# Layer 1 attention: first value block as three float32r products, normalisation on ScalarE, the token tile in two halves

## The chip, the cores and the metric

The kernel runs on one core of one Trainium2 chip, in one launch. The time is the device time of that core in microseconds (us), and the number compared is a median over runs. Before the change it is 2091.49 us, the median of three runs (2091.32 to 2092.57).

## The reference

A decoder trunk of two layers on 256 tokens of 2048 float32 features. Layer 0 mixes tokens with a block-sparse attention (at this length plain causal attention, 16 heads of 128), layer 1 with a latent attention ("MLA"), and each is followed by a gated feed-forward block with a short causal convolution:

```python
for i in range(DEPTH):                      # DEPTH = 2
    h = rms_norm(x, attn_norm[i])
    y = moba_attention(h, ...) if i == 0 else mla_attention(h, ...)
    x = x + y
    h = rms_norm(x, ffn_norm[i])
    x = x + conv_glu_ffn(h, ...)

def mla_attention(h, ...):
    cq = rms_norm(h @ wq_a, g_qa)                 # 512
    q = (cq @ wq_b).reshape(B, S, H, NOPE + RD)   # 16 heads, 128 + 64
    ckv = rms_norm(kv_a[..., :512], g_kva)        # kv_a = h @ wkv_a
    kv = (ckv @ wkv_b).reshape(B, S, H, NOPE + VD)
    s = (q_nope @ k_nope + q_rope @ k_rope) * scale   # per head, causal
    p = softmax(s)
    o = p @ v                                     # this product is changed
    return o.reshape(B, S, H * VD) @ wo
```

What the change touches is the softmax's last step (the division by the row sums) and the product of the probabilities with v, in layer 1 only, and where some tiles lie in SBUF.

## The kernel before

**Weights.** All weights stream through one class, `Stream`. A piece is 128x512 float32; 1480 pieces arrive in 370 units of up to four by transfers on SyncE's queue (L71), three units ahead. For each piece ScalarE makes a rounded float32r part `whi` (L104) and VectorE the rest `wlo = raw - whi` (L105). Five buffers of each exist, and in the steady state a piece is split four quanta before TensorE uses it.

**Quanta.** The program is a list of quanta, one for each weight piece: TensorE's products of that piece. A product of two float32 matrices is done as three float32r products (high by high, high by low, low by high). In token-major quanta (`tok_major`, L237) six products of 512 columns use the activations as the stationary operand and the weights as the moving one. In feature-major quanta (`feat_major`, L263 to L265) twelve products of 256 columns have it the other way round.

**Order.** The order is written out by hand. The last loop (L1086 to L1092) issues for each quantum: the splits of the piece four quanta on, the quantum's products, then `leading` work (values, then transposes of heads), then the `side` work planned for that quantum, in the order in which it was planned. Every engine runs its instructions in that order, so a late instruction delays all that stands behind it on its engine.

**Layer 1 attention.** Four groups of four heads. Each group has projections of four quanta each (k, q, v; the first group q, the rotary part, k, v), then four heads, three quanta apart. `Head.plan` (L554) puts a head's steps on quanta: at q `scores` on TensorE and `biased` on VectorE (mask and row maximum), at q+1 `exps` on ScalarE with row sums, at q+2 `normal` (a VectorE reciprocal, L509, and two VectorE multiplications, L511), at q+6 `turn` (three TensorE transposes, L519) and `turned` (the copy out of PSUM), at q+9 `values` (TensorE) and `parted` (the output as high and low part, L551 and L552, in `oT`). For the last head the steps come at q+5 and q+7.

In layer 1 before the change, `turned` is one ScalarE copy of 128x384 (L525) and `values` is two float32 products: 256 columns for the first block of keys (L544) and 128 columns for the second (L545). A float32 product stands in the trace as two MATMULs. Layer 0 (`parts=True`) already has the other form: `turned` is a float32r copy of the first block (L531), a float32 copy of the second (L532) and a VectorE subtraction for the low part (L533); `values` is three float32r products (L462 to L464) and one float32 product (L542).

**Tiles.** The normalised tokens are one tile `h` of 16 rows of 512 (high and low part). In layer 1, once the projections have read it, its place is taken by `room`, one tile with the queries, the keys, the values and the rotary key `kr` of layer 1. The values come from PSUM by two ScalarE copies of 128x512 for a group (L619, in `evac_values`).

Of the kernel before, what the change touches and what calls it, by code (L numbers as in the profile page):

```python
# [10 lines left out]
F32 = mybir.dt.float32  # L11
F32R = mybir.dt.float32r
BF16 = mybir.dt.bfloat16
AF = mybir.ActivationFunctionType
ALU = mybir.AluOpType
PSUM = bass.MemoryType.PSUM

P = 128
S = 256
D = 2048  # L20
NT = S // P
KD = D // P
# [28 lines left out]
H_START = 8  # L51


class Stream:
# [55 lines left out]

    def take(self, i):
        return self.parts.pop(i)


@with_exitstack
def trunk(ctx: ExitStack, tc: tile.TileContext, a, out):
    nc = tc.nc
    const = ctx.enter_context(tc.tile_pool(name="const", bufs=1))
    keep = ctx.enter_context(tc.tile_pool(name="keep", bufs=1))
# [8 lines left out]
    mm = nc.tensor.matmul  # L128
# [35 lines left out]
    att_pool = att.enter_context(tc.tile_pool(name="att", bufs=2))  # L164
# [50 lines left out]
    def at(q, f, *args):  # L215
        side.setdefault(q, []).append((f, args))
# [7 lines left out]
    def add(f, *args):  # L224
        quanta.append((f, args))
        return len(quanta) - 1
# [41 lines left out]
    class Norm:  # L268
# [3 lines left out]
        def __init__(self, gain_col, spread):  # L272
            self.gain_col, self.spread = gain_col, spread
            self.h, self.sq = None, {}

        def high(self, j):
            if self.h is None:
                t = keep.tile([P, KD * 2 * S + 64], F32R, name="h")
                self.h = t[:, H_START : H_START + KD * 2 * S].rearrange("p (k s) -> p k s", k=KD)
            g = par[:, self.gain_col + j : self.gain_col + j + 1]  # L280
            nc.scalar.activation(self.h[:, j, :S], xT[:, j, :], AF.Copy, scale=g)  # L281

# [177 lines left out]
    def three(o, w_hi, w_lo, m_hi, m_lo, start, stop):  # L460

        mm(o, w_hi, m_hi, start=start, stop=False)  # L462
        mm(o, w_hi, m_lo, start=False, stop=False)  # L463
        mm(o, w_lo, m_hi, start=False, stop=stop)  # L464


    class Head:
        def __init__(self, h, qT, kT, v, i, oT, scale, rope=None, parts=False):
            self.h, self.qT, self.kT, self.v, self.i = h, qT, kT, v, i
            self.oT, self.scale, self.rope, self.parts = oT, scale, rope, parts  # L470

        def scores(self):
            sc = ps_sc.tile([P, 512], F32, name="sc")
# [34 lines left out]
        def normal(self):  # L508
            nc.vector.reciprocal(self.st[:, 6:8], self.st[:, 4:6])  # L509
            for c, n, k in ((0, P, 0), (P, S, 1)):  # L510
                nc.vector.tensor_scalar(  # L511
                    self.s[:, c : c + n], self.s[:, c : c + n], self.st[:, 6 + k : 7 + k], None,
                    op0=ALU.mult,
                )
# [5 lines left out]
            self.tp = tp  # L520

        def turned(self):
            if not self.parts:
                self.pT = att_pool.tile([P, 3 * P], F32, name="pT", bufs=2)
                nc.scalar.copy(self.pT, self.tp[:, : 3 * P])  # L525
                return

            self.pT = att_pool.tile([P, 2, S], F32R, name="pT", bufs=2)
            self.pT1 = att_pool.tile([P, P], F32, name="pT1", bufs=2)
            hi, lo = self.pT[:, 0], self.pT[:, 1]  # L530
            nc.scalar.copy(hi, self.tp[:, :S])  # L531
            nc.scalar.copy(self.pT1, self.tp[:, S : 3 * P])  # L532
            nc.vector.tensor_tensor(lo, self.tp[:, :S], hi.bitcast(F32), op=ALU.subtract)  # L533

        def values(self):
            o = ps_sc.tile([P, 512], F32, name="sc")
            v = self.v()
            vs = slice(self.i * P, (self.i + 1) * P)
            if self.parts:
                v0, v1 = v  # L540
                three(o[:, :S], v0[:, 0, vs], v0[:, 1, vs], self.pT[:, 0], self.pT[:, 1], True, False)
                mm(o[:, P:S], v1[:, vs], self.pT1, start=False, stop=True)  # L542
            else:
                mm(o[:, :S], v[:, 0, vs], self.pT[:, :S], start=True, stop=False)  # L544
                mm(o[:, P:S], v[:, 1, vs], self.pT[:, S:], start=False, stop=True)  # L545
            self.o = o

        def parted(self):
# [22 lines left out]
    env = {}  # L571
# [32 lines left out]
    def evac_parts(state, key, scale):  # L604
        v0, v1 = env[key]
        hi, lo = v0[:, 0], v0[:, 1]
        first_, second = (state["acc"][t][:, :512] for t in range(NT))
        r = scale()
        nc.scalar.activation(hi, first_, AF.Copy, scale=r[:, 0:1])
        nc.vector.scalar_tensor_tensor(  # L610
            lo, first_, r[:, 0:1], hi.bitcast(F32), op0=ALU.mult, op1=ALU.subtract
        )
        nc.scalar.activation(v1, second, AF.Copy, scale=r[:, 1:2])

    def evac_values(state, key, scale):
        for t in range(NT):
            dst, src = env[key][:, t, :], state["acc"][t][:, :512]
            if scale is None:
                nc.scalar.copy(dst, src)  # L619
            else:  # L620
                nc.scalar.activation(dst, src, AF.Copy, scale=scale()[:, t : t + 1])

    def plan_heads(q, hs, key, step, out=None, late=0, wide=False):

# [30 lines left out]
    for g in range(4):  # L655
        for kind in "qkv":
            state = {"first": g == 0 and kind == "q"}
            for kt in range(KD):
                q = add(tok_major, state, lambda: n1.h, kt, KD - 1)
# [228 lines left out]

    def kr_rotate(t):
        if t == 0:  # L890
            env["krr"] = att_pool.tile([P, NT, 2, 64], F32, name="krr", bufs=1)
        x = env["ckv"][:, t, 512:]
        nc.vector.scalar_tensor_tensor(
            x, x, env["kvr"][:, 2 * t + 1 : 2 * t + 2], gains[:, G_KR : G_KR + 64],
            op0=ALU.mult, op1=ALU.mult,
        )
        ct = tab[:, T_LC + t * 64 : T_LC + (t + 1) * 64]
        st = tab[:, T_LS + t * 64 : T_LS + (t + 1) * 64]
        t1 = att_pool.tile([P, 64], F32, name="kro1", bufs=2)
        t2 = att_pool.tile([P, 64], F32, name="kro2", bufs=2)  # L900
        nc.vector.tensor_tensor(t1, x, ct, op=ALU.mult)
        nc.vector.tensor_tensor(t2[:, :32], x[:, 32:], st[:, :32], op=ALU.mult)
        nc.vector.tensor_tensor(t2[:, 32:], x[:, :32], st[:, 32:], op=ALU.mult)
        for i in range(2):
            nc.vector.tensor_tensor(env["krr"][:, t, i], t1, t2, op=ALU.add)
# [56 lines left out]
    for r in range(4):  # L962
        state = {}
        for kq in range(4):
            q = add(lambda t_hi, t_lo, n, st=state, kq=kq: feat_major(
                st, lambda: n3.h, 4 * kq, KD - 1, kq == 0, t_hi, t_lo, n))
# [52 lines left out]
    for half in range(2):  # L1019
        state = {}  # L1020
        for kt in range(KD):
            q = add(tok_major, state, lambda: n3.h, kt, KD - 1)
# [1 line left out]
        at(q + (0 if half else 1), kva_squares, half)  # L1024

    def open_room():
        t = keep.tile([P, KD * 2 * S + 64], F32, name="room", tag="h")
        env["room"] = t[:, : 32 * S].rearrange("p (k s) -> p k s", k=32)
        env["kr"] = [env["room"][:, 28 + i] for i in range(2)]

    at(q, open_room)
    at(q, kva_rstd)
# [4 lines left out]
    for t in range(NT):  # L1037
        at(q + 9 + t, kr_rotate, t)
    at(q + 13, kr_turn)

    def mla_tiles(g):
        i = 4 * (g % 2)
        env["qT", g] = env["room"][:, i : 4 + i]
        env["kT", g] = env["room"][:, 8 + i : 12 + i]
        i = 4 * (g % 3)
        env["v", g] = env["room"][:, 16 + i : 20 + i].rearrange("p (t c) s -> p t (c s)", t=NT)

    for g in range(4):
        for kind in "kqv" if g else "qrkv":
            if kind == "r":  # L1050
                rotary_queries(1, (6, 8, 10, 11, 12, 15, 16, 18, 19, 21, 22, 24, 25, 27, 28, 31, 32))
                continue
            state = {}
            for kt in range(4):
                q = add(tok_major, state, lambda kind=kind: env["cqT" if kind == "q" else "ckvT"], kt, 3)
            if kind == ("k" if g else "q"):
                at(q, mla_tiles, g)
            if kind == "v":
                at(q, evac_values, state, ("v", g), None)
            else:  # L1060
                q_q = q
                hs = Heads(state, 4, P, None, 0, None, (lambda: cq["scale"]) if kind == "q" else None,
                           C_GQN if kind == "q" else C_GKN)
                plan_heads(q, hs, ("qT" if kind == "q" else "kT", g), 1, wide=(g, kind) == (0, "q"))
        for i in range(4):
            hd = Head(
                4 * g + i, lambda g=g: env["qT", g], lambda g=g: env["kT", g], lambda g=g: env["v", g],
                i, lambda: env["oT"], MLA_SCALE,
                rope=lambda h=4 * g + i: (env["qrT"][:, h // 2, :], env["kr"][h % 2]),
            )  # L1070
            q0 = q_q + 11 + 3 * i
            last = g == i == 3
            hd.plan(q0, q0 + (7 if last else 9), q0 + 5 if last else None)
# [132 lines left out]
```

## Time and profile before

| | before |
|---|---|
| median of 3 runs | 2091.49 us |
| the profiled execution's own time | 2092.06 us |
| its span, first to last instruction | 2090.2 us |
| granted TensorE clock | 1.000 |
| TensorE busy | 2084.2 us, 16716 matmuls |
| VectorE busy | 1405.6 us |
| ScalarE busy | 1132.1 us |
| layer 1, first to last product of probabilities with v | 1214.4 to 1311.5 us |

A row of the page or of a group of instructions names the line, the engine, the operation, output and input tiles, the shape and the count, then the busy time and the mean of one. A row of the timeline has the start, the time covered by the instructions merged in it, the engine, line and operation, the count, and in square brackets how long the engine had been idle and what ended that. Matmuls are pipelined, so the time that a product takes of TensorE is read from start to start of neighbours, not from its own duration. PE is TensorE, DVE is VectorE, ACT is ScalarE, POOL is GpSimd, SPq is the queue of SyncE.

### The profile page before, as it was taken

The numbers are of one execution on the slowest core, as the hardware profiler recorded it, in microseconds if no ns is written. First come the engines' busy times: TensorE is split into PE (matmuls) and PEld (weight loads), VectorE is DVE, ScalarE is ACT, GpSimd is POOL, SyncE is SP. The second block draws the span as 40 slices with busy tenths as digits, with TensorE's granted clock in tenths as the row PEclk, the third lists the DMA queues.
The fourth block names the chain that finished last, engine by engine and source line by source line (L and its number), as shares of the span: only waits on it lengthen the run. The fifth ranks groups of instructions, "written<-read, shape, count | busy, mean of one in ns | idle before, by whom it ended". The sixth has DMA issues, their size and how long they took to land.

```text
span 2090.2 us, 42176 instructions
## 1 busy us (share of the span) xinstructions
PE 2084.2 (100%) x16716; PEld 2014.5 (96%) x16716; DVE 1405.6 (67%) x3081; ACT 1132.1 (54%) x2206; POOL 46.4 (2%) x37
## 2 busy tenths in 40 slices
PE   9999999999999999999999999999999999999999
PEld 7888889999999999999999889999999999999999
DVE  6777776776666766655556886776676666765554
ACT  6555555555555555545455665655555555544443
POOL 0000000000000000000000210000000000000000
PEclk9999999999999999999999999999999999999999
DMA  7454445455555555555554533455555555555553
GB/s 273 162 181 172 169 163 201 183 194 190 202 187 197 196 189 201 194 191 196 193 195 159 195 122 122 182 195 190 201 188 196 197 189 201 189 201 209 197 205 131
DMA packets 59381, 391.81 MB, mean 187 GB/s; under 512 B 6960, under 2 KB 10032, under 8 KB 13232
## 3 DMA queue, kind: packets, MB, share of 16 engines
q1 hardware_dynamic: 59040, 388.87, 52.0%
q8 instruction: 130, 2.13, 0.4%
q14 instruction: 67, 0.55, 0.1%
q10 hardware_dynamic: 144, 0.26, 0.1%
HBM read 387.01 MB, written 2.10 MB: 186 GB/s over the span
## 4 chain that ended last, share of the span: by engine, by line
PE 99%; DMA 0%; SPq 0%; DVE 0%; ACT 0%; issue 0%
PE acc L263 26%; PE acc L265 26%; PE acc L264 26%; PE acc L237 17%; PE tp L447 1%; PE sc L484 1%; PE sc L487 1%; PE tp L519 1%; PE sc L544 0%; DMA xT<-in_xT 0%; PE sc L463 0%; PE sc L464 0%; PE sc L462 0%; PE sc L542 0%; PE sc L479 0%; PE sc L545 0%
## 5 line engine op out<-in xcount | busy, mean ns | idle before, releaser
L105 DVE TENSOR_TENSOR wlo<-raw,whi 128x512 fp32r<-128x512 f32 (+1 forms) x1480 | 1001.1, 684 | 393.3 <-ACT whi L104 390.7
L104 ACT CAST whi<-raw 128x512 fp32r<-128x512 f32 (+1 forms) x1479 | 872.1, 614 | 460.3 <-PE acc L264 212.2
L263 PE MATMUL acc<-h,whi 128*128 128x256 f32 x2880 | 796.3, 276 | 0.0
L265 PE MATMUL acc<-h,wlo 128*128 128x256 f32 x2880 | 795.9, 276 | 0.0
L264 PE MATMUL acc<-h,whi 128*128 128x256 f32 x2880 | 795.9, 276 | 0.0
L263 PEld LDWEIGHTS acc<-h,whi 128*128 128x128 f32 x2880 | 540.8, 188 | 0.0
L264 PEld LDWEIGHTS acc<-h,whi 128*128 128x128 f32 x2880 | 540.8, 188 | 0.0
L265 PEld LDWEIGHTS acc<-h,wlo 128*128 128x128 f32 x2880 | 540.8, 188 | 0.0
L265 PE MATMUL acc<-a,wlo 128*128 128x256 f32 x1408 | 389.1, 276 | 0.0
L263 PE MATMUL acc<-a,whi 128*128 128x256 f32 x1408 | 389.1, 276 | 0.0
L264 PE MATMUL acc<-a,whi 128*128 128x256 f32 x1408 | 389.0, 276 | 0.0
L237 PE MATMUL acc<-whi,h 128*128 128x512 f32 (+1 forms) x896 | 272.3, 380 | 0.7 <-ACT h L281 0.5
L263 PEld LDWEIGHTS acc<-a,whi 128*128 128x128 f32 x1408 | 264.4, 188 | 0.0
L264 PEld LDWEIGHTS acc<-a,whi 128*128 128x128 f32 x1408 | 264.4, 188 | 0.0
L265 PEld LDWEIGHTS acc<-a,wlo 128*128 128x128 f32 x1408 | 264.4, 188 | 0.0
L237 PEld LDWEIGHTS acc<-whi,h 128*128 128x128 f32 x896 | 164.7, 188 | 31.0 <-ACT h L281 1.1
L237 PE MATMUL acc<-wlo,h 128*128 128x512 f32 (+1 forms) x448 | 169.0, 378 | 0.4 <-DVE wlo L105 0.4
L263 PE MATMUL acc<-oT,whi 128*128 128x256 f32 x512 | 143.7, 281 | 0.0
L265 PE MATMUL acc<-oT,wlo 128*128 128x256 f32 x512 | 141.8, 277 | 0.0
L264 PE MATMUL acc<-oT,whi 128*128 128x256 f32 x512 | 141.7, 277 | 0.0
L753 DVE TENSOR_TENSOR g<-acc,rstd_b 128x256 f32<-128x256 f32 x88 | 37.5, 426 | 125.4 <-PE acc L265 122.4
L760 ACT ACTIVATE c<-g,par 128x256 f32<-128x256 f32 x88 | 53.1, 603 | 108.0 <-DVE g L753 108.0
(161 smaller groups left out, 1595.4 us busy)
## 6 DMA issues: line engine op xcount, KB each, us to landing
raw<-in_ffn_gu SPq DMA_DIRECT2D x176, 1024.0 KB, 4.8
raw<-in_ffn_down SPq DMA_DIRECT2D x88, 1024.0 KB, 4.8
raw<-in_moba_wk SPq DMA_DIRECT2D x16, 1024.0 KB, 4.8
raw<-in_moba_wv SPq DMA_DIRECT2D x16, 1024.0 KB, 4.8
raw<-in_moba_wo SPq DMA_DIRECT2D x16, 1024.0 KB, 4.8
raw<-in_mla_wo SPq DMA_DIRECT2D x16, 1024.0 KB, 4.8
raw<-in_moba_wq SPq DMA_DIRECT2D x13, 1024.0 KB, 4.8
raw<-in_mla_wkv_a SPq DMA_DIRECT2D x8, 576.0 KB, 3.6
```

The source lines that it names most:

```text
L104: self.nc.scalar.copy(hi[:, :n], w)
L105: self.nc.vector.tensor_tensor(lo[:, :n], w, hi[:, :n].bitcast(F32), op=ALU.subtract)
L237: mm(state["acc"][t][:, :n], src[:, kt, c : c + P], (t_lo if part == 1 else t_hi)[:, :n], start=kt == 0 and part == 0, stop=kt == k_last a ...
L263: mm(o, w_hi, src[:, kt, :S], start=first and k == 0, stop=False, skip_group_check=True)
L264: mm(o, w_hi, src[:, kt, S:], start=False, stop=False, skip_group_check=True)
L265: mm(o, w_lo, src[:, kt, :S], start=False, stop=kt == k_last, skip_group_check=True)
L447: nc.tensor.transpose(tp[:, (i * NT + t) * P : (i * NT + t + 1) * P], flat[:, t, c : c + P], ident)
L484: mm(o, qT[:, i, q0 : q0 + P], kT[:, i, :n], start=True, stop=self.rope is None)
L487: mm(o, qr[:, q0 : q0 + P], kr[:, :n], start=False, stop=True)
L519: nc.tensor.transpose(tp[:, c * P : (c + 1) * P], self.s[:, c * P : (c + 1) * P], ident)
L753: nc.vector.tensor_tensor(self.g[:, 2:], self.gate["acc"][:, :S], self.norm.rstd_b, op=ALU.mult)
L760: nc.scalar.activation(self.c, self.g[:, 2:], AF.Identity, bias=par[:, cb : cb + 1], scale=self.cw(2))
```

## The change

- In layer 1 `normal` keeps its VectorE reciprocal, but the two multiplications (128x128 and 128x256) are done by ScalarE, as an activation Copy with the reciprocal as scale.
- `turned` has layer 0's form in both layers: two ScalarE copies and one VectorE subtraction in place of one ScalarE copy. In layer 1 the two parts of the first block lie in a new tile `vroom`, in one of two places by the head's parity.
- `values` has layer 0's form in both layers: three float32r products and one float32 product.
- The values of layer 1 come out of PSUM by `evac_parts`: a float32r copy (ScalarE), a subtraction for the low part (VectorE) and a float32 copy of the second block (ScalarE). Before it was two ScalarE copies.
- The tile `h` becomes two tiles `h0` and `h1` of eight rows each, each with its own 64 spare elements. In layer 1 the queries and keys take the place of `h0` (float32), the values and the turned probabilities that of `h1` (float32r). The rotary key and the second block of values get tiles of their own, and `krr` shares the place of `cacc`.

```diff
+class Halves:
+    def __init__(self, tiles):
+        self.tiles = tiles
+    def __getitem__(self, at):
+        p, k, s = at
+        return self.tiles[k // 8][p, k % 8, s]
...
-                t = keep.tile([P, KD * 2 * S + 64], F32R, name="h")
-                self.h = t[:, H_START : H_START + KD * 2 * S].rearrange("p (k s) -> p k s", k=KD)
+                n = KD // 2 * 2 * S
+                tiles = [keep.tile([P, n + 64], F32R, name=f"h{i}") for i in range(2)]
+                self.h = Halves([
+                    t[:, H_START : H_START + n].rearrange("p (k s) -> p k s", k=KD // 2) for t in tiles
+                ])
...
+            self.latent = rope is not None
...
             for c, n, k in ((0, P, 0), (P, S, 1)):
+                if self.latent:
+                    s = self.s[:, c : c + n]
+                    nc.scalar.activation(s, s, AF.Copy, scale=self.st[:, 6 + k : 7 + k])
+                    continue
                 nc.vector.tensor_scalar(
...
         def turned(self):
-            if not self.parts:
-                self.pT = att_pool.tile([P, 3 * P], F32, name="pT", bufs=2)
-                nc.scalar.copy(self.pT, self.tp[:, : 3 * P])
-                return
-            self.pT = att_pool.tile([P, 2, S], F32R, name="pT", bufs=2)
+            if self.latent:
+                i = 12 + 2 * (self.h % 2)
+                self.pT = env["vroom"][:, i : i + 2]
+            else:
+                self.pT = att_pool.tile([P, 2, S], F32R, name="pT", bufs=2)
             self.pT1 = att_pool.tile([P, P], F32, name="pT1", bufs=2)
             hi, lo = self.pT[:, 0], self.pT[:, 1]
             nc.scalar.copy(hi, self.tp[:, :S])
...
-            if self.parts:
-                v0, v1 = v
-                three(o[:, :S], v0[:, 0, vs], v0[:, 1, vs], self.pT[:, 0], self.pT[:, 1], True, False)
-                mm(o[:, P:S], v1[:, vs], self.pT1, start=False, stop=True)
-            else:
-                mm(o[:, :S], v[:, 0, vs], self.pT[:, :S], start=True, stop=False)
-                mm(o[:, P:S], v[:, 1, vs], self.pT[:, S:], start=False, stop=True)
+            v0, v1 = v
+            three(o[:, :S], v0[:, 0, vs], v0[:, 1, vs], self.pT[:, 0], self.pT[:, 1], True, False)
+            mm(o[:, P:S], v1[:, vs], self.pT1, start=False, stop=True)
...
         first_, second = (state["acc"][t][:, :512] for t in range(NT))
+        if scale is None:
+            nc.scalar.copy(hi, first_)
+            nc.vector.tensor_tensor(lo, first_, hi.bitcast(F32), op=ALU.subtract)
+            nc.scalar.copy(v1, second)
+            return
...
     def open_room():
-        t = keep.tile([P, KD * 2 * S + 64], F32, name="room", tag="h")
-        env["room"] = t[:, : 32 * S].rearrange("p (k s) -> p k s", k=32)
-        env["kr"] = [env["room"][:, 28 + i] for i in range(2)]
+        n = 16 * S
+        t = keep.tile([P, n + 64], F32, name="room", tag="h0")
+        env["room"] = t[:, :n].rearrange("p (k s) -> p k s", k=16)
+        t = keep.tile([P, n + 64], F32R, name="vroom", tag="h1")
+        env["vroom"] = t[:, :n].rearrange("p (k s) -> p k s", k=16)
+        t = att_pool.tile([P, 2, S], F32, name="kr", bufs=1)
+        env["kr"] = [t[:, i] for i in range(2)]
...
-                at(q, evac_values, state, ("v", g), None)
+                at(q, evac_parts, state, ("v", g), None)
```

More of the change, by code (lines that the diff above doesn't have):

```diff
@@ L613, in evac_parts @@
         nc.scalar.activation(v1, second, AF.Copy, scale=r[:, 1:2])
[L615 to L621, printed above, removed]
     def plan_heads(q, hs, key, step, out=None, late=0, wide=False):
@@ L890, in kr_rotate @@
         if t == 0:
-            env["krr"] = att_pool.tile([P, NT, 2, 64], F32, name="krr", bufs=1)
+            env["krr"] = att_pool.tile([P, NT, 2, 64], F32, name="krr", tag="cacc", bufs=1)
         x = env["ckv"][:, t, 512:]
@@ L1045, in mla_tiles @@
         i = 4 * (g % 3)
-        env["v", g] = env["room"][:, 16 + i : 20 + i].rearrange("p (t c) s -> p t (c s)", t=NT)
+        env["v", g] = (
+            env["vroom"][:, i : i + 4].rearrange("p (t c) s -> p t (c s)", t=2),
+            att_pool.tile([P, 512], F32, name="v1", bufs=3),
+        )
     for g in range(4):
```

## The prediction

> **What bounds the kernel now.** I read the page's shares and its chain first, then TensorE's waits, then the stage that changes, engine by engine. Of the page:
>
> ```profile
> PE 2084.2 (100%) x16716; PEld 2014.5 (96%) x16716; DVE 1405.6 (67%) x3081; ACT 1132.1 (54%) x2206; POOL 46.4 (2%) x37
> ...
> PE 99%; DMA 0%; SPq 0%; DVE 0%; ACT 0%; issue 0%
> ```
>
> TensorE is busy throughout, and the chain that ended last is 99% TensorE. All of TensorE's waits in the whole span:
>
> ```profile
> PE sc L174 <- DVE zeros L171: 1.2, 1, 1.2
> PE acc L237 <- ACT h L281: 0.5, 1, 0.5
> PE acc L237 <- DVE wlo L105: 0.4, 2, 0.2
> PE acc L237 <- ACT whi L104: 0.2, 1, 0.2
> ```
>
> That is 2.3 us of 2090.2. So the time moves by what TensorE has to stream, and it grows where ScalarE or VectorE deliver too late. There is almost no stall left to remove. The stage in question, from the first values evacuation until the projections end, has this row (columns: busy time and instructions of PE, PEld, DVE, ACT, POOL, then clock, DMA share, GB/s), and these waits are the two that matter in it:
>
> ```profile
> 1186.00:1262.00 76.00, 76.00 (x405) 64.92 (x404) 63.93 (x278) 52.84 (x123) 15.06 (x7) 1.00 0.37 129
> ```
>
> ```profile
> ACT s L502 <- DVE sst L498: 10.4, 8, 3.8
> DVE wlo L105 <- ACT whi L104: 7.6, 8, 2.0
> ```
>
> TensorE never idles at a granted clock of 1.00; VectorE has 12.1 us free of 76, ScalarE 23.2, and the two already wait for each other.
>
> **The change, part by part.**
>
> *The product, on TensorE.* The first two rows and the third are a layer 1 head before (float32, then its second block, then the next work); the others are a layer 0 head, which has the new form already:
>
> ```profile
> 1214.41 0.59 PE L544 MATMUL sc<-pT,room 128*128 128x256 f32 x2
> 1214.84 0.39 PE L545 MATMUL sc<-pT,room 128*128 128x128 f32 x2
> 1215.06 0.49 PE L519 MATMUL tp<-ident,s 128*128 128x128 f32 x3
> ```
>
> ```profile
> 98.51 0.28 PE L462 MATMUL sc<-pT,v 128*128 128x256 f32 x1
> 98.62 0.28 PE L463 MATMUL sc<-pT,v 128*128 128x256 f32 x1
> 98.74 0.28 PE L464 MATMUL sc<-pT,v 128*128 128x256 f32 x1
> 98.86 0.39 PE L542 MATMUL sc<-pT,v 128*128 128x128 f32 x2
> ```
>
> From start to start the float32 product takes 1214.84 - 1214.41 = 0.43 us and the three float32r products 98.86 - 98.51 = 0.35 us. The second block costs the same in both (0.22 us, L545 to L519). So a head gains 0.08 us, and 16 heads gain 1.3 us. This lies on the path. The weight loads that go from two to three are within the 0.35 us.
>
> The Trainium skill would make this larger: "FP8 and Floating Point Precision", section TensorE Precision Notes, has true FP32 as four passes through the array, so three passes would save a quarter, an estimate of 0.11 us a head and 1.7 us in all. The trace has 0.35 for three, not 0.32; I take the trace.
>
> *Normalisation, from VectorE to ScalarE.* ScalarE does work of the same shapes, SBUF to SBUF with one operand per partition, in the exponentials:
>
> ```profile
> 1199.25 0.41 ACT L502 ACTIVATE s<-s,sst 128x128 f32<-128x128 f32 x1 [0.57 <-DVE sst L498]
> 1199.56 0.19 ACT L502 ACTIVATION_READ_ACCUMULATOR s<-s,sst 128x1 f32 x1
> 1199.65 0.49 ACT L502 ACTIVATE s<-s,sst 128x256 f32<-128x256 f32 x1
> 1200.05 0.19 ACT L502 ACTIVATION_READ_ACCUMULATOR s<-s,sst 128x1 f32 x1
> ```
>
> Next start minus start gives 0.31 + 0.40 = 0.71 us a head, 11.4 us for 16, added on ScalarE. VectorE loses this:
>
> ```profile
> 1209.67 0.16 DVE L509 RECIPROCAL sst<-sst 128x2 f32<-128x2 f32 x1
> 1209.86 0.55 DVE L511 TENSOR_SCALAR s<-s,sst 128x128 f32<-128x128 f32 x2
> 1210.33 0.69 DVE L105 TENSOR_TENSOR wlo<-raw,whi 128x512 fp32r<-128x512 f32 x1
> ```
>
> It is 0.47 us a head, 7.5 us in all. Neither is on TensorE's path. The cost in time is the new wait: ScalarE now stands still until VectorE has reached L509, and behind it on ScalarE stand the casts `whi`, behind those on VectorE `wlo`, and behind those TensorE. The transposes that need the result come four quanta later, so they are not late.
>
> *Turning the probabilities, and the values.* ScalarE goes from one copy to two, VectorE gets a subtraction, and a group's values get one too. The rows of the old form and of layer 0's (durations min, median, max):
>
> ```profile
> L525 ACT COPY pT<-tp x16: 478/479/483, 1209.6 to 1307.8; 128x384 f32<-128x384 f32 x16
> ```
>
> ```profile
> L531 ACT CAST pT<-tp x16: 354/372/373, 94.0 to 315.0; 128x256 fp32r<-128x256 f32 x16
> L532 ACT COPY pT<-tp x16: 257/272/274, 94.3 to 315.2; 128x128 f32<-128x128 f32 x16
> L533 DVE TENSOR_TENSOR pT<-tp,pT x16: 414/424/426, 94.6 to 315.5; 128x256 fp32r<-128x256 f32 x16
> ```
>
> ScalarE: 0.372 + 0.272 - 0.479 = +0.17 us a head. VectorE: +0.42 us a head. For the four groups' low parts I take the 0.69 us of a subtraction of the same size (the L105 row above), 2.8 us in all; the evacuations on ScalarE stay two a group. In sum ScalarE gets 16 x 0.88 = 14 us more, VectorE 16 x (0.42 - 0.47) + 2.8 = 2 us more. In the 76 us window with nine normalisations, eight turned heads and three groups, ScalarE goes from 52.8 to about 60.6 us, VectorE from 63.9 to about 65.2. Neither fills.
>
> *Is a piece late for TensorE?* Two places decide, and I shift them by hand. The first is after the first group's values, where VectorE is tightest:
>
> ```profile
> 1189.72 0.69 DVE L399 TENSOR_TENSOR qk<-qk,hr 128x512 f32<-128x512 f32 x1 [0.26 <-POOL hr L394]
> ...
> 1192.12 0.69 DVE L105 TENSOR_TENSOR wlo<-raw,whi 128x512 fp32r<-128x512 f32 x1
> ```
>
> ```profile
> 1193.88 0.39 PE L237 MATMUL acc<-wlo,cqT 128*128 128x512 f32 x1
> ```
>
> This `wlo` is ready at 1192.81 and used at 1193.88, 1.07 us ahead. The new subtraction (0.69) goes in before L399, whose own wait of 0.26 swallows part: 0.43 us later, 0.6 us still in hand. The second place is the second head's normalisation:
>
> ```profile
> 1208.13 1.05 ACT L619 COPY room<-acc 128x512 f32<-128x512 f32 x2
> 1209.09 0.62 ACT L104 CAST whi<-raw 128x512 fp32r<-128x512 f32 x1
> ```
>
> ```profile
> 1213.27 0.39 PE L237 MATMUL acc<-wlo,ckvT 128*128 128x512 f32 x1
> ```
>
> Here `wlo` (1210.33, quoted above) is ready at 1211.02 and used at 1213.27, 2.25 us ahead. Afterwards: VectorE reaches the reciprocal some 0.4 to 0.9 us later (carried lag and the second group's subtraction, less the first head's 0.47), so near 1210.6; ScalarE, done with L619 at about 1209.4, waits until 1210.8, normalises until 1211.5 and casts until 1212.1; `wlo` follows until 1212.8. That leaves 0.5 us. A wait of a few tenths here or in the next heads is possible and I put 0.2 us in the sum. Its bounds: below, 0, since TensorE hardly waits now; above, what the first rival gives.
>
> *The tiles.* Two tiles in place of one add 64 elements (256 bytes), and all that is allocated behind moves. No instruction is added. The part buffers are 576 elements apart and rotate, and `h` starts at element 8 while `a` starts at 0, yet the means agree:
>
> ```profile
> L263 PE MATMUL acc<-h,whi 128*128 128x256 f32 x2880 | 796.3, 276 | 0.0
> ...
> L263 PE MATMUL acc<-a,whi 128*128 128x256 f32 x1408 | 389.1, 276 | 0.0
> ```
>
> So I take 0. The halves are written when their last readers are done, and those are earlier quanta, as before. The transfers keep their order on SyncE's queue; a `raw` buffer comes free later by the shift of `wlo`, about 1 us, against three units (twelve pieces) of lead. POOL's clearing of `kr` and the shared place of `krr` wait for readers long done.
>
> *Sum.* The profiled execution took 2092.06 us, 1.9 us more than its span and 0.57 above the median. Against it: 2092.06 - 1.3 + 0.2 = 2091.0; against the median, 2091.49 - 1.1 = 2090.4 us.
>
> **Rivals.**
>
> *ScalarE's second wait reaches TensorE (slower).* Each head makes ScalarE wait for VectorE twice. Price in the window, on ScalarE: 52.84 busy + 9 x 0.88 new + 10.4 waits for `sst` as now + up to 1.2 us at each of nine reciprocals (the walk above gave 1.4 at its worst) = 82 us where 76 are there. If nothing of that overlaps, TensorE stalls 6 us, and the time is 2091.49 - 1.3 + 6 = 2096.2 us. It decides from a stall of 5.5 us on (4.2 us are 0.2%). For it speaks that VectorE and ScalarE are coupled through `whi`; against it, that a late ScalarE shortens its own waits for `sst`, and that leads of only about one microsecond at the start of the stage hold now without a stall. "ScalarE: Activation LUTs" of the Trainium skill, Rules for kernel authors, says to use VectorE, not ScalarE, for a multiplication; here 0.71 us against 0.47 us agrees with it, and the sum does not change as long as ScalarE has the time.
>
> *No gain on TensorE.* If loads of three operands or a late part stretch the product to the old 0.43 us, 1.3 us goes: about 2091.7 us. Against it stand layer 0's rows.
>
> *Four passes (faster).* By the row of 0.43 alone, a quarter off is 0.11 us a head, 1.7 us: about 2089.8 us.
>
> *The moved tiles cost or gain.* If one nanosecond were added to each of the 14,400 feature-major products (L263 to L265), this would be 14 us, 2104.6 us; as a gain it would be 2076. The equal means speak against both.
>
> **How the numbers follow.** 4.2 us (0.2%) is about what a measurement of this kernel can tell from no change. Forecast, 2089.5 to 2091.5: 0.74. No gain: 0.08. Four passes: 0.05. ScalarE's wait: 0.09, of which 0.06 lies above the bound. Moved tiles: 0.04, three of them slower. So faster by over 0.2% has 0.01 (rounded up to 0.02 for what I don't see), slower 0.09, within 0.2% the rest, 0.89. The range takes in forecast, both neighbours and most of the stall: 2089.0 to 2094.0 us.
>
> **What would show it.** The three products take 0.35 us from start to start at the place of L544; TensorE's busy time falls by about 1.3 us. In TensorE's waits a new row of `wlo` or `whi` between 1186 and 1262 us, if any, stays under 1 us. ScalarE shows a new wait, s for the reciprocal, of under 1.5 us each, and 14 us more busy time. The forecast is wrong if that wait appears again behind TensorE with more than 2 us, or if feature-major products outside the stage leave 276 ns.

## The result

The changed kernel takes 2094.10 us (median of 22 runs, 2093.29 to 2096.06) where the kernel before takes 2091.81 (22 runs, 2091.05 to 2093.51). The ratio is 1.0012, with a 95% interval of 1.0006 to 1.0017: 0.12% or 2.3 us slower. That is within the 0.2% that the prediction took for no change, but the interval lies above 1, where the forecast was 1.1 us faster, and 2094.1 is above the range. The profiled execution took 2094.61 us, its span is 2092.8 us.

The page after, shares and chain:

```profile
PE 2084.1 (100%) x16732; PEld 2013.9 (96%) x16732; DVE 1404.8 (67%) x3069; ACT 1143.3 (55%) x2254; POOL 46.2 (2%) x37
...
PE 95%; DVE 3%; ACT 2%; issue 0%; DMA 0%; SPq 0%; ACTq 0%
```

The chain was 99% TensorE and is 95% now. Nearly all of the rest is one unbroken stretch, in which it runs through VectorE and ScalarE alone for 95 us before it comes back to TensorE. Its two ends (start, us, engine, output):

```profile
1174.83 0.27 issue
1175.10 1.02 ACT qr L390 x2
...
1269.38 0.43 DVE oT L567
1269.80 0.04 issue
1269.85 0.39 PE acc L275
```

In the kernel before, no part of the chain from 1150 to 1320 us is on these two engines. TensorE's waits after:

```profile
PE tp L461 <- ACT room L472: 2.4, 2, 1.5
PE sc L185 <- DVE zeros L182: 1.2, 1, 1.2
PE acc L248 <- DVE wlo L105: 0.7, 3, 0.2
PE acc L275 <- DVE oT L567: 0.4, 1, 0.4
PE acc L248 <- ACT h L295: 0.2, 1, 0.2
```

Each row gives the total in us, the number of waits and the longest. The first row is new, and so is the fourth. `tp` is the transposes' tile in PSUM, which TensorE writes and ScalarE empties, and L472 is ScalarE's copy of transposed keys or queries out of it (`turned_out`, L458 before). The stage that the prediction looked at, same window:

```profile
1186.00:1262.00 76.00, 73.64 (x400) 62.57 (x399) 60.79 (x259) 57.35 (x145) 14.89 (x7) 1.00 0.34 119
```

TensorE's busy time falls from 76.00 to 73.64 us at an unchanged clock: two waits, both here. The first of them, on TensorE:

```profile
1207.95 0.49 PE L538 MATMUL tp<-ident,s 128*128 128x128 f32 x3
...
1209.59 0.60 PE L461 MATMUL tp<-ident,qk 128*128 128x128 f32 x4
...
1211.18 0.40 PE L248 MATMUL acc<-whi,ckvT 128*128 128x512 f32 x1
1213.04 0.66 PE L461 MATMUL tp<-ident,qk 128*128 128x128 f32 x4 [1.46 <-ACT room L472]
```

and what ScalarE did meanwhile:

```profile
1207.38 0.60 ACT L104 CAST whi<-raw 128x512 fp32r<-128x512 f32 x1
1209.68 0.80 ACT L528 ACTIVATE s<-s,sst 128x128 f32<-128x128 f32 x2 [1.70 <-DVE sst L524]
1210.39 0.56 ACT L624 CAST vroom<-acc 128x512 fp32r<-128x512 f32 x1
1210.85 0.58 ACT L626 COPY v<-acc 128x512 f32<-128x512 f32 x1
1211.33 0.63 ACT L104 CAST whi<-raw 128x512 fp32r<-128x512 f32 x1
1211.85 0.38 ACT L550 CAST vroom<-tp 128x256 fp32r<-128x256 f32 x1
1212.11 0.28 ACT L551 COPY pT<-tp 128x128 f32<-128x128 f32 x1
1212.27 0.72 ACT L472 ACTIVATE room<-tp,par 128x512 f32<-128x512 f32 x1
```

ScalarE stands 1.70 us for VectorE's reciprocal (L524), then normalises (L528, 0.71 us), evacuates the values, casts a piece, copies the probabilities out, and only then makes the copy L472, which ends at 1212.99. TensorE's next transposes start 0.05 us later. VectorE stands too: behind its reciprocal comes the low part of the values, which needs ScalarE's cast, and ScalarE makes that only after the normalisation:

```profile
1209.43 0.16 DVE L524 RECIPROCAL sst<-sst 128x2 f32<-128x2 f32 x1
1210.98 0.69 DVE L625 TENSOR_TENSOR vroom<-acc,vroom 128x512 fp32r<-128x512 f32 x1 [1.40 <-ACT vroom L624]
```

So here the two engines wait for each other in turn. The chain has VectorE alone from 1202.19 until the reciprocal: ScalarE stands because VectorE has that much to do ahead of it. The same copy in the kernel before (L458) and the transposes around it:

```profile
1209.39 0.60 PE L447 MATMUL tp<-ident,qk 128*128 128x128 f32 x4
1211.22 0.60 PE L447 MATMUL tp<-ident,qk 128*128 128x128 f32 x4
```

```profile
1210.03 0.69 ACT L458 ACTIVATE room<-tp,par 128x512 f32<-128x512 f32 x1
```

There it ended at 1210.72, 0.50 us ahead of the next transposes. That trace lies 0.20 us earlier at this place (1209.39 against 1209.59), so the copy begins 1212.27 - 1210.03 - 0.20 = 2.04 us later after the change: more than the 0.50 us in hand.

The row's 1.46 us counts from the modelled end of the product at 1211.18 (0.40 us), but such products follow each other 0.23 us from start to start. From start to start the place costs 1213.04 - 1211.18 - 0.23 = 1.63 us. The second wait, on the copy L472 again, and the third, on the low part of an output (`oT`):

```profile
1242.24 0.66 PE L461 MATMUL tp<-ident,qk 128*128 128x128 f32 x4 [0.89 <-ACT room L472]
...
1269.85 0.39 PE L275 MATMUL acc<-oT,whi 128*128 128x256 f32 x1 [0.38 <-DVE oT L567]
```

Read from start to start in the same way, the second place costs 1.06 us and the third 0.54 us, 3.2 us for all three.

### The profile page after: what moved, and what is told of

The parts are those of the page before. It is cut to its first block, busy times and chain, and to the rows that moved or that the text cites. A ratio compares the mean times of both kernels' runs of the same rounds, so it can differ in the third digit from the quotient of the medians.

```text
span 2092.8 us, 42259 instructions
## 1 busy us (share of the span) xinstructions
PE 2084.1 (100%) x16732; PEld 2013.9 (96%) x16732; DVE 1404.8 (67%) x3069; ACT 1143.3 (55%) x2254; POOL 46.2 (2%) x37
## 4 chain that ended last, share of the span: by engine, by line
PE 95%; DVE 3%; ACT 2%; issue 0%; DMA 0%; SPq 0%; ACTq 0%
PE acc L275 26%; PE acc L274 26%; PE acc L276 26%; PE acc L248 14%; DVE wlo L105 1%; DVE junk L395 0%; PE tp L461 0%; ACT whi L104 0%; PE tp L538 0%; DVE qk L413 0%; DMA xT<-in_xT 0%; ACT s L517 0%; ACT s L528 0%; PE sc L560 0%; PE sc L477 0%
```

## The experiments

Each experiment has 11 runs and is compared with runs of the kernel before that were taken beside it: 2091.73 us for the first four (33 runs), 2091.96 us for the last three (27 runs). For the changed kernel 2094.10 stands against 2091.81.

**Normalisation back on VectorE.** From the changed kernel:

```diff
-                if self.latent:
-                    s = self.s[:, c : c + n]
-                    nc.scalar.activation(s, s, AF.Copy, scale=self.st[:, 6 + k : 7 + k])
-                    continue
```

> The changed kernel with the multiplications of the normalisation back on VectorE, all else as changed. Theory 'standing ScalarE' (ScalarE stands at each reciprocal, so the copies out of the transposes' PSUM buffers behind it come late and TensorE waits for a free buffer): the two TensorE waits of 2.4 us together are gone, the cheaper product is left, about 1.2 us faster than before: 2090.6 us. Rival 'work or tiles' (the extra copies and subtractions, or the moved tiles, cost the time): stays near 2094 us.

Measured 2090.56 us, 1.2 us less than before, ratio 0.9994 (0.9986 to 1.0003). All of TensorE's waits in this run:

```profile
PE sc L185 <- DVE zeros L182: 1.2, 1, 1.2
PE acc L248 <- DVE wlo L105: 0.4, 2, 0.2
```

The waits are gone with that one step, so three products, longer copies, subtractions and tiles together bring about the 1.2 us of the cheaper product, though the interval of this run alone takes in no change. Moving the normalisation, with the rest of the change in place, costs 2.3 + 1.2 = 3.5 us: the slowest run here (2091.80) lies below the fastest of the changed kernel (2093.29), and the three waits of 3.2 us nearly account for it.

**The same work, one quantum later.** From the changed kernel, the reciprocal stays on q+2 and `weighted` holds ScalarE's two multiplications:

```diff
             at(q + 2, self.normal)
+            if self.latent:
+                at(q + 3, self.weighted)
```

> The changed kernel with the reciprocal on quantum q+2 as now and ScalarE's two multiplications one quantum later, q+3. ScalarE does the same work, but VectorE has passed the reciprocal when it gets there. Theory 'standing ScalarE': its waits for the reciprocal fall from 15.7 us (16 times) to under 5, no TensorE wait for a transpose buffer is left, 2090.6 to 2091.0 us. Rival 'amount of work' (14 us more work on ScalarE is what delays the copies): stays near 2094 us.

Measured 2090.62 us, ratio 0.9995 (0.9986 to 1.0003). The stage and ScalarE's waits for VectorE's row sums, maxima and reciprocals in this run:

```profile
1186.00:1262.00 76.00, 76.00 (x419) 65.33 (x417) 64.68 (x268) 60.59 (x152) 15.28 (x8) 1.00 0.35 125
```

```profile
ACT s L517 <- DVE sst L513: 7.4, 11, 2.0
ACT s L532 <- DVE sst L524: 0.4, 1, 0.4
```

ScalarE is busy 60.59 of 76 us and TensorE is busy all the time. So the amount of work costs nothing that shows here; L532 waits once for the reciprocal, 0.4 us in all, where the changed kernel's L528 waits 16 times:

```profile
ACT s L528 <- DVE sst L524: 15.7, 16, 1.7
```

**The wait without the work.** From the kernel with the normalisation on VectorE, ScalarE copies the two reciprocals into dead columns at the old place:

```diff
             nc.vector.reciprocal(self.st[:, 6:8], self.st[:, 4:6])
+            if self.latent:
+                nc.scalar.copy(self.st[:, 0:2], self.st[:, 6:8])
```

> The changed kernel with the multiplications back on VectorE, but ScalarE copies the two reciprocals (128x2, into dead columns) at the same place in its order: the wait without the work. Theory 'standing ScalarE': TensorE waits for transpose buffers as in the changed kernel, 2093 to 2094 us. Rival 'amount of work': 2090.6 to 2091.2 us, no TensorE wait.

Measured 2091.98 us, ratio 1.0002 (0.9993 to 1.0011): 1.4 us above the kernel without the wait (2090.56 us), which was measured beside it. TensorE waits at the first of the two places only, and ScalarE waits at all 16 reciprocals:

```profile
PE tp L461 <- ACT room L472: 1.3, 1, 1.3
```

```profile
ACT sst L526 <- DVE sst L524: 14.8, 16, 1.6
```

The time lies between the theory's 2093 to 2094 us and the rival's 2090.6 to 2091.2. The wait alone makes a stall of 1.4 us, the work without the wait makes none, and both together cost 3.5 us: the 0.71 us of multiplications count only when they come behind the wait. The theory had taken the wait for all of it.

**Only the normalisation moved.** From the kernel before, the multiplications on ScalarE and nothing else:

```diff
+                if self.rope is not None:
+                    s = self.s[:, c : c + n]
+                    nc.scalar.activation(s, s, AF.Copy, scale=self.st[:, 6 + k : 7 + k])
+                    continue
                 nc.vector.tensor_scalar(
```

> The kernel before with only the multiplications moved to ScalarE; product, values, copies and tiles as before. Theory 'standing ScalarE': TensorE waits 2 to 3.5 us for transpose buffers and nothing is gained on the product: 2094 to 2095.3 us. Rival 'it takes the longer copies and subtractions as well': 2091.8 to 2092.5 us.

Measured 2092.81 us, ratio 1.0005 (0.9996 to 1.0014), 1.1 us above before and less than expected; it lies between the two expectations, and the interval takes in no change. One group of transposes waits in layer 1:

```profile
1212.37 0.66 PE L447 MATMUL tp<-ident,qk 128*128 128x128 f32 x4 [0.74 <-ACT pT L529]
```

Its releaser is the single copy of the probabilities (L529), not the keys' copy behind it. From start to start this place costs 0.90 us (the product before it starts at 1211.24). So the step alone costs about 1 us, and 3.5 us together with the rest of the change, which makes TensorE wait nowhere by itself. That the longer copies and subtractions do this is likely, but no run separates them.

**Only the tiles moved.** From the kernel before, `h` in halves, `room` and `vroom` in their places (values still float32), `kr` in its own tile, `krr` with `cacc`:

```diff
+        t = keep.tile([P, n + 64], F32, name="room", tag="h0")
...
+        t = keep.tile([P, n + 64], F32, name="vroom", tag="h1")
...
+        t = att_pool.tile([P, 2, S], F32, name="kr", bufs=1)
```

> The kernel before with only the tiles moved: h in two halves, queries and keys in the place of the first, values (still float32) in that of the second, the rotary key in a tile of its own, krr in the place of cacc. Theory 'standing ScalarE': no cost, 2091.5 to 2092 us, no TensorE wait in layer 1. Rival 'moved tiles': part of the 3.5 us between the changed kernel and the one with the normalisation on VectorE cannot be the tiles (both have them), but the gain of 1.2 us could be; then 2090.6 us here.

Measured 2092.16 us, ratio 1.0000 (0.9991 to 1.0009), and no wait of TensorE in layer 1. The tiles neither cost nor gain as far as this can tell.

**The transposes' banks strictly in turn.** In the changed kernel the transposes at 1213.04 wait for L472, the copy of the transposes just before them (1209.59), so both use one PSUM buffer (bank) of the two; the same holds for those at 1239.36 and 1242.24. With only the normalisation moved they wait for the copy of the probabilities instead, which lie in the other bank. That they alternate in the kernel before as well, as the expectation says, no trace can show, since nothing waits there. From the changed kernel:

```diff
+    def tp_tile():
+        turn_of[0] ^= 1
+        return ps_tp.tile([P, 512], F32, name="tp", tag=f"tp{turn_of[0]}")
```

> The changed kernel with the two PSUM banks of the transposes taken strictly in turn. In the changed kernel, at both places where TensorE waits, two transposes of a key or query pair in a row use the same bank, so the second waits for the copy (L472) of the first; in the kernel before they alternate there. Rival 'shared bank': with alternation the two waits (2.4 us) go, 2091.5 to 2092 us. Theory 'standing ScalarE': the other bank is held by the turned probabilities, whose last reader on VectorE ends at 1213.0 and 1242.3 us, no earlier than L472, so TensorE waits as long, now for those copies: 2093.8 to 2094.4 us.

Measured 2094.12 us, ratio 1.0011 (1.0002 to 1.0020):

```profile
PE tp L467 <- DVE vroom L558: 2.4, 2, 1.4
```

TensorE waits as long, now for VectorE's subtraction of the probabilities (L558, L552 in the changed kernel), which stands behind the same late copies. The shared bank decides whom TensorE waits for, not how long.

**The values ahead of the normalisation.** From the changed kernel:

```diff
-                at(q, evac_parts, state, ("v", g), None)
+                first_in(q, 1, evac_parts, state, ("v", g), None)
```

> The changed kernel with the evacuation of a group's values issued ahead of the normalisation of the same quantum, not behind it, so that ScalarE's two copies of 128x512 (0.94 us) run while it would stand at the reciprocal. Theory 'standing ScalarE, with the copies stacked behind it': VectorE's low part of the values now comes before the reciprocal and eats about 0.6 us of that, so each of the two TensorE waits shortens by 0.3 to 0.5 us: about 2093.2 to 2093.6 us. Rival 'only the reciprocal's wait counts, not what stands behind': 2094 us.

Measured 2093.24 us, ratio 1.0008 (0.9999 to 1.0016). The two waits on TensorE, and ScalarE around the first:

```profile
1213.00 0.66 PE L461 MATMUL tp<-ident,qk 128*128 128x128 f32 x4 [1.05 <-ACT room L472]
1241.85 0.66 PE L461 MATMUL tp<-ident,qk 128*128 128x128 f32 x4 [0.54 <-ACT room L472]
```

```profile
1208.24 0.57 ACT L624 CAST vroom<-acc 128x512 fp32r<-128x512 f32 x1
1208.72 0.57 ACT L626 COPY v<-acc 128x512 f32<-128x512 f32 x1
1210.62 0.80 ACT L528 ACTIVATE s<-s,sst 128x128 f32<-128x128 f32 x2 [1.33 <-DVE sst L524]
```

The copies now run while ScalarE would stand. The waits shorten from 1.46 to 1.05 and from 0.89 to 0.54 us, by 0.4 us each, and the third, for `oT`, is gone. So what stands behind the wait on ScalarE counts, as the theory says. The traces carry this; the times of the two kernels' runs overlap (2092.68 to 2095.42 here, 2093.29 to 2096.06 for the changed kernel).

Two versions come out below both kernels, 2090.56 and 2090.62 us, but the 1.1 to 1.2 us under the kernel before is within their intervals.

## Why the prediction was wrong

*The product* came out as worked out. After, in the same view as before:

```profile
1216.31 0.28 PE L476 MATMUL sc<-vroom 128*128 128x256 f32 x1
1216.43 0.28 PE L477 MATMUL sc<-vroom 128*128 128x256 f32 x1
1216.55 0.28 PE L478 MATMUL sc<-vroom 128*128 128x256 f32 x1
1216.67 0.38 PE L560 MATMUL sc<-pT,v 128*128 128x128 f32 x2
```

It is 0.36 us where 0.35 stood in the sum and 0.43 was before; 16 heads give 1.1 us, and the run with the normalisation on VectorE shows 1.2 us in the time. The quarter off that the four-pass rival expected is not seen.

*ScalarE's and VectorE's work* was near. In the window ScalarE's 60.6 us became 60.59 us in the run one quantum later. That close a match is partly luck, since the window of that run holds 152 ScalarE instructions where 123 + 26 were counted on. Over the whole span ScalarE has 11.2 us more in the changed kernel (1143.3 against 1132.1) where 14 stood, and VectorE 0.8 less where 2 more stood. *The tiles* were right at 0: no wait and no change of the time beyond the interval.

*"Is a piece late for TensorE?"* is the step that failed: its 0.2 us measured 3.5 us. It followed only the weight pieces, `whi` and `wlo`, and no product waits for those between 1186 and 1262 us; the 0.7 us of such waits after (0.6 before) all lie in the first 100 us. The delay reached TensorE by another road, which the sum put at nothing. A transpose needs a PSUM buffer that has been emptied, and ScalarE empties it, behind the wait. The prediction asked whether the data of the transposes come in time ("four quanta later, so they are not late") and not whether their place is free. Two groups of transposes of keys or queries are one quantum apart, not four (1.83 us in the kernel before, 1209.39 to 1211.22), and the copy between them had 0.50 us in hand.

The walk also had the order on ScalarE wrong: it let the values' evacuation (L619) go first and the normalisation follow, and the program issues the normalisation first, as the timeline shows. VectorE reached the reciprocal at 1209.43, not near 1210.6, and yet ScalarE stood 1.70 us instead of 1.4, and the evacuation and everything behind it came 2 us later. The sign that the prediction named for being wrong, more than 2 us of this wait behind TensorE, is what the first row of TensorE's waits shows (2.4 us).

*The first rival*, that ScalarE's second wait reaches TensorE, is what happened, with its trigger right and the way (through `whi` and `wlo`) not. Its price of 6 us assumed that nothing overlaps; the stall of 3.5 us is below its point of 5.5, so the time stayed within 0.2%. It had a chance of 0.09, and by the prediction's own numbers 0.06 of that lay above 0.2%, so the range to 2094.0 did not take in "most of the stall", as it says, but left most of it out. That ScalarE would shorten its waits for `sst` as it got later was right, but made up for only part of the 15.7 us of new waits: 13.1 us in the changed kernel from 1186 to 1312 us against 20.4 in the one with the normalisation on VectorE (16.4 in the kernel before):

```profile
ACT s L517 <- DVE sst L513: 13.1, 15, 1.6
```

```profile
ACT s L517 <- DVE sst L513: 20.4, 15, 3.8
```

*The third wait*, 0.38 us for `oT`, ends the same chain: at 1266.43 ScalarE has stood 1.36 us for a reciprocal, the evacuation and a cast follow, and only then the outputs' parts (L566 on ScalarE, L567 on VectorE). It is absent with the normalisation on VectorE, one quantum later, or behind the evacuation of the values.

*What stays open:* how much of the 3.5 us the longer copies and how much the subtractions add to the 1.1 us of the step alone was not separated.

## What to carry to other kernels

When a step moves to an engine that must then wait for the engine it left, list everything behind the wait on the in-order queue, and for each item ask who needs not only its data but the buffer that it empties. Issue the dependent half later in the queue instead of next to its producer: here one quantum later made the same work free (2094.1 to 2090.6 us). A busy share far from full on both engines (here 57 and 61 of 76 us) does not say that such a wait is harmless.

## What the runs showed that was not expected

Which PSUM bank a transpose uses differs between the changed kernel and the one with only the normalisation moved, without any edit to the pool; what decides it was not separated. With the banks strictly in turn the name of the releaser changed and not the time (2094.12 against 2094.10 us). And an idle time of TensorE in a row is short of what the place costs: 1.46 us in the row, 1.63 us from start to start, since the product before it is drawn 0.40 us long while its successors follow after 0.23.
